# Values of a dilated attention in six chunks of 512 weight columns, queries and keys laid out by head, softmax minimum in one operation

## The chip, the cores and the metric

The kernel runs on one core of a Trainium2 chip. The metric is the device time of one execution in microseconds (us), lower is better. Engines are called as in the profile: PE (TensorE, its weight load apart as PEld), DVE (VectorE), ACT (ScalarE), POOL (GpSimd), SP (SyncE, which issues nearly all transfers).

## The reference, cut to what matters

Four half layers on 256 tokens of width 1024: a mixer of neighbourhood and latent attention, an MLP, a mixer of dilated attention (the odd mixer), an MLP. The change touches the odd mixer alone:

```python
DIL_PAIRS = ((128, 1), (512, 4), (2048, 16)); DIL_HEADS = 16; HEAD_DIM = 64

def dilated_attention(q, k, v):            # b, s, 3 groups, 16 heads, 64
    offsets = [jnp.arange(-(w // 2), w // 2 + 1, d) for (w, d) in DIL_PAIRS]
    ...
        for gi in range(g):
            sc = einsum(q_blk[:, :, gi], k_sel) * scale      # keys at the group's offsets
            sc = jnp.where(valid, sc, NEG_INF)
            m = jnp.max(sc, axis=-1, keepdims=True); e = jnp.exp(sc - m); z = sum(e)
            outs.append(einsum(e / z, v_sel)); lses.append(m + jnp.log(z))
        wgt = softmax(stack(lses), axis=0)
        out = sum(wgt * stack(outs), axis=0)

def odd_mixer(xn, w_in, w_o, cos_f, sin_f):
    hcat = (xn @ w_in).reshape(b, s, DIL_GROUPS, 3, DIL_HEADS, HEAD_DIM)
    q = apply_rope(hcat[:, :, :, 0], cos_f, sin_f)
    k = apply_rope(hcat[:, :, :, 1], cos_f, sin_f)
    v = hcat[:, :, :, 2]
    return dilated_attention(q, k, v) @ w_o
```

The weighting by the groups' sums makes the three groups of a head one softmax over the keys of all three, which is how the kernel computes it.

## The kernel before, in words

All weights come in as float32 and are split on the chip: ACT casts a piece to its high part `whi` (L176), DVE subtracts it for the low part `wlo` (L177). A product is then either three matmuls (`mm3`, L180 to L182, tokens as the stationary side) or, for queries and keys, a pair of one 512-column and one 256-column matmul per 128 input features (`mm2`, L186 and L187). A weight is one transfer on SP's queue into one of 4 buffers `raw`, split in 4 pieces, two weights ahead of its use, into one of 3 split buffers. The list `specs` fixes the order of the weights.

The odd mixer works in 8 units of two heads. A unit has three weights of queries and keys (`w_oqk`: first the queries and keys of group 0, q0, then the queries of groups 1 and 2, q12, then their keys, k12; four steps of 8 matmuls each) and two weights of values (`w_ov`: four steps of 12 matmuls each, 384 columns: two heads in three groups). After each product of queries or keys the halves are joined (ACT copy L193, DVE add L194); after each second one comes the rotation: four transfers `sw<-qk` on SP, multiplications on DVE (L850, L851), and the sum (L853, or L856 for q12 and k12). Values are scaled out of PSUM in L818 (DVE) and L821, L822 (ACT).

The attention of unit u-1 is laid between the steps of unit u by `weave`, which deals a list of side steps evenly between the main steps. Its parts are: `scores` (L201 for group 0, L881 for the small products of groups 1 and 2), inside it the product with the values of unit u-2 (`mix`, L917 and L922), then for each of 2 token tiles and 2 heads a softmax, and four `turn`s (three transposes L902 and a copy `pts`, L904, on DVE or ACT). A softmax is: scaled minimum with the mask on DVE (L889, the minimum is of the negated scores), exponential on ACT (L893), reciprocal on DVE (L894), scaling on ACT (L895). The small products of group g go to the score bank `ss[i, g]`, so a head's scores lie in three places, and its minimum is taken in three operations, each of which begins with the result of the one before:

```python
for n, (o, cs) in enumerate(((ss[i, j][:, 0:T], slice(0, T)), (ss[i, 0][:, at(j)], at(0)), (ss[i, 1][:, at(j)], at(1)))):
    nc.vector.tensor_tensor_reduce(out=sn[:, cs], in0=o, in1=mask[:, i, cs], ...,
                                   scalar=mn[:, n - 1:n] if n else 3e38, accum_out=mn[:, n:n + 1])
```

The attention of unit 7 lies between the steps of the output projection. PSUM is 8 banks, 4 named `w` (scores, transposes) and 4 named `acc` (products of weights, mix). The order of instructions on each engine is not the program's: a scheduler rearranges it by a model of its own.

Of the kernel before, what the change touches and what calls it, by code (L numbers as in the profile page):

```python
# [16 lines left out]
F32 = mybir.dt.float32  # L17
# [22 lines left out]
WPARTS = 4  # L40
NORM_PRIO = 300


@with_exitstack
def trunk(ctx, tc, a, out):
# [739 lines left out]
    def odd(op, xT, s):  # L785
# [8 lines left out]
        def unit_tiles(u):  # L794
            d = {}
            for n, shape, dt in (("q0", [P, 2, 2, T], F32R), ("q12", [P, 2, T], F32), ("k12", [P, 2, T], F32),
                                 ("v0", [P, NT, P], F32), ("v12", [P, 4, P], F32)):
                d[n] = op.tile(shape, dt, tag=n, name=n, bufs=2)
            return d

        def value_steps(d):

            wt, acc = [], {}

            def gemm(i, half):
                if len(wt) <= half:
                    wt.append(weight())
                if half == 0:
                    acc[i] = bank("acc")
                pq = acc[i]  # L810
                wh, wl = wt[half]
                for k in range(4):
                    ws = slice(k * 384, k * 384 + 384)
                    kk = 4 * half + k
                    mm3(pq[:, 0:384], xh[:, kk, tok(i)], xl[:, kk, tok(i)], wh[:, ws], wl[:, ws], kk == 0, kk == KT - 1)
            def out(i):
                pq, ri = acc[i], column(r[0], i)
                nc.vector.tensor_scalar(d["v0"][:, i, :], pq[:, 0:P], ri, None, ALU.mult)  # L818
                for c in range(2):
                    rows = slice(64 * c, 64 * c + 64)  # L820
                    nc.scalar.activation(d["v12"][0:64, 2 * i + c, :], pq[rows, P:2 * P], AF.Copy, scale=ri[rows])  # L821
                    nc.scalar.activation(d["v12"][64:P, 2 * i + c, :], pq[rows, 2 * P:3 * P], AF.Copy, scale=ri[rows])  # L822

            return [lambda i=i, h=h: gemm(i, h) for i in range(NT) for h in range(2)], [lambda i=i: out(i) for i in range(NT)]
# [34 lines left out]

        def all_values(d):  # L860
            g, o = value_steps(d)
            return [g[0], lambda: run_all([g[1], o[0]]), g[2], lambda: run_all([g[3], o[1]])]

        turned = {}

        def attention(u, d, other, pause=2):
# [4 lines left out]
            def scores():  # L871
                ss = {(i, j): bank("w") for i in range(NT) for j in range(2)}
                for i in range(NT):
                    two_heads([ss[i, j][:, 0:T] for j in range(2)], d["q0"], tok(i))
                at = lambda n: slice(T + 64 * n, T + 64 * n + 64)
                for i in range(NT):
                    for j in range(2):
                        for c in range(2):
                            for g in range(2):
                                pb, own = slice(64 * g, 64 * g + 64), slice(i * P + 64 * c, i * P + 64 * c + 64)  # L880
                                nc.tensor.matmul(ss[i, g][64 * c:64 * c + 64, at(j)], d["q12"][pb, j, own], d["k12"][pb, j, own],  # L881
                                                 start=True, stop=True)
                other()
                for i in range(NT):
                    for j in range(2):
                        sn, pp = scratch([384], "sn"), scratch([384], "pp")
                        mn, z, rz = (work.tile([P, n], F32, tag=v, name=v, bufs=4) for v, n in (("dmn", 3), ("dz", 1), ("drz", 1)))
# [20 lines left out]

        def mix(u, d, out_tag):
            pvo = bank(out_tag)  # L910
            for i in range(NT):
                pts = [turned.pop((u, i, j)) for j in range(2)]
                at = i * P
                for kk in range(NT):
                    for j in range(2):
                        cs = slice(64 * j, 64 * j + 64)
                        nc.tensor.matmul(pvo[cs, tok(i)], d["v0"][:, kk, cs], pts[j][:, kk, :], start=kk == 0, stop=False)  # L917
                for c in range(2):
                    qs = slice(64 * c, 64 * c + 64)
                    for j in range(2):  # L920
                        cs = slice(64 * j, 64 * j + 64)
                        nc.tensor.matmul(pvo[cs, at + 64 * c:at + 64 * c + 64], d["v12"][:, 2 * i + c, cs], pts[j][:, 2, qs],  # L922
                                         start=False, stop=c == 1)
            split(*halves(mixed[u // 4][:, u % 4]), pvo[:, 0:T])

        d, nd = unit_tiles(0), unit_tiles(1)
        v0, v_out = value_steps(d)
        run_all(v0)
        r = [rstd(s)]
# [7 lines left out]
        run_all(first[2:])  # L937
        weave(qk_steps(nd) + all_values(nd), attention(0, d, lambda: None, 3), 3)
        for u in range(2, 8):
            pd, d, nd = d, nd, unit_tiles(u)  # L940
            side = attention(u - 1, d, lambda: mix(u - 2, pd, "acc"))

            weave(qk_steps(nd) + all_values(nd), side + [lambda: mix(6, d, "acc")] if u == 7 else side)
        accs, wo = open_accs(), {}
        side = attention(7, nd, lambda: None) + [lambda: mix(7, nd, "w")]
        weave([f for k in range(6) for f in out_steps(accs, mixed, wo, k)], side)
# [54 lines left out]
def _layout(i):  # L1001
# [14 lines left out]
    wo = i["od_w_in"][0].reshape(D, 3, 3, 8, 2, HD)  # L1016
    cols = [(0, 0, 0), (0, 0, 1), (0, 1, 0), (0, 1, 1), (1, 0, 0), (2, 0, 0),
            (1, 0, 1), (2, 0, 1), (1, 1, 0), (2, 1, 0), (1, 1, 1), (2, 1, 1)]
    qk = np.stack([wo[:, g, s, :, j] for g, s, j in cols], 2).reshape(KT, P, 8, 3, 2, P)
    d["w_oqk"] = f(qk.transpose(2, 3, 1, 4, 0, 5).reshape(8, 3, P, WCH))  # L1020
    d["w_ov"] = f(wo[:, :, 2].reshape(2, 4, P, 3, 8, P).transpose(4, 0, 2, 1, 3, 5).reshape(8, 2, P, 4 * 384))
    d["w1"] = f(i["mlp_w1"].reshape(2, KT, P, 16, 256).transpose(0, 3, 2, 1, 4).reshape(2, 16, P, WCH))
# [35 lines left out]
```

## Time and profile before

| what | value |
|---|---|
| median of 3 runs | 744.25 us (744.05 to 745.09) |
| the profiled execution, its own time | 743.78 us |
| its span in the trace | 742.0 us |
| PE busy | 733.4 us (99%) |
| PEld busy | 644.5 us (87%) |
| DVE busy | 551.5 us (74%) |
| ACT busy | 461.7 us (62%) |
| POOL busy | 6.0 us (1%) |
| HBM read | 127.68 MB |

The span is what the trace covers; the execution's own time has 1.78 us more around it. Busy shares are means over all four half layers. The odd mixer lies about between 290 and 575 us of the span.

### The profile page before, as it was taken

The numbers are of one execution on the slowest core, as the hardware profiler recorded it, in microseconds if no ns is written. First come the engines' busy times: TensorE is split into PE (matmuls) and PEld (weight loads), VectorE is DVE, ScalarE is ACT, GpSimd is POOL, SyncE is SP. The second block draws the span as 40 slices with busy tenths as digits, with TensorE's granted clock in tenths as the row PEclk, the third lists the DMA queues.
The fourth block names the chain that finished last, engine by engine and source line by source line (L and its number), as shares of the span: only waits on it lengthen the run. The fifth ranks groups of instructions, "written<-read, shape, count | busy, mean of one in ns | idle before, by whom it ended". The sixth has DMA issues, their size and how long they took to land.

```text
span 742.0 us, 12701 instructions
## 1 busy us (share of the span) xinstructions
PE 733.4 (99%) x4764; PEld 644.5 (87%) x4764; DVE 551.5 (74%) x1248; ACT 461.7 (62%) x1032; POOL 6.0 (1%) x16
## 2 busy tenths in 40 slices
PE   8999999999999999999999999999999999999996
PEld 6998998888888888989899899898998888888885
DVE  6798869666665666998888988888769665665664
ACT  7679867554554546758776766877667544554541
POOL 0100000000000000000000000000000000000000
PEclk9999999999999999999999999999999999999999
DMA  8976334555555554574655555457553546455501
GB/s 296 336 207 220 117 118 164 190 208 182 179 206 185 177 178 150 198 257 150 211 195 185 177 190 189 167 175 240 201 199 126 215 170 208 171 189 190 184 24 57
DMA packets 28108, 136.88 MB, mean 184 GB/s; under 512 B 4496, under 2 KB 7056, under 8 KB 14992
## 3 DMA queue, kind: packets, MB, share of 16 engines
q1 hardware_dynamic: 27760, 135.81, 53.6%
q8 instruction: 37, 0.61, 0.3%
q10 hardware_dynamic: 288, 0.28, 0.1%
q14 instruction: 23, 0.19, 0.1%
HBM read 127.68 MB, written 1.05 MB: 173 GB/s over the span
## 4 chain that ended last, share of the span: by engine, by line
PE 94%; ACT 1%; DMA 1%; issue 1%; DVE 1%; SPq 0%; POOLq 0%; POOL 0%; DVEq 0%
PE w L186 16%; PE acc L180 14%; PE acc L181 14%; PE acc L182 14%; PE acc L186 12%; PE w L187 8%; PE acc L187 6%; PE w L902 1%; PE w L201 1%; PE acc L917 1%; PE w L714 1%; PE w L730 1%; DMA raw<-in_w_v 1%; PE w L881 1%; PE w L180 1%
## 5 line engine op out<-in xcount | busy, mean ns | idle before, releaser
L177 DVE TENSOR_TENSOR wlo<-raw,whi 128x512 fp32r<-128x512 f32 (+3 forms) x488 | 304.0, 663 | 71.5 <-ACT whi L176 70.0
L176 ACT CAST whi<-raw 128x512 fp32r<-128x512 f32 (+3 forms) x488 | 264.3, 601 | 80.3 <-issue 70.1
L186 PE MATMUL w<-xT,whi 128*128 128x512 f32 x512 | 179.4, 394 | 0.0
L186 PE MATMUL acc<-xT,whi 128*128 128x512 f32 x384 | 137.2, 401 | 0.0
L187 PE MATMUL w<-xT,wlo 128*128 128x256 f32 x512 | 132.9, 280 | 0.0
L186 PEld LDWEIGHTS w<-xT,whi 128*128 128x128 f32 x512 | 93.6, 187 | 18.3
L187 PEld LDWEIGHTS w<-xT,wlo 128*128 128x128 f32 x512 | 96.1, 188 | 5.5
L187 PE MATMUL acc<-xT,wlo 128*128 128x256 f32 x384 | 99.7, 280 | 0.0
L180 PE MATMUL acc<-whi,h 128*128 128x512 f32 x250 | 98.4, 393 | 0.0
L181 PE MATMUL acc<-wlo,h 128*128 128x512 f32 x250 | 97.8, 391 | 0.0
L182 PE MATMUL acc<-whi,h 128*128 128x512 f32 x250 | 97.4, 390 | 0.0
L186 PEld LDWEIGHTS acc<-xT,whi 128*128 128x128 f32 x384 | 69.9, 188 | 12.7
L193 ACT COPY up<-w 128x256 f32<-128x256 f32 x64 | 23.8, 372 | 88.5 <-PE w L186 88.5
L187 PEld LDWEIGHTS acc<-xT,wlo 128*128 128x128 f32 x384 | 72.2, 188 | 3.7
L194 DVE TENSOR_TENSOR up<-up,w 128x256 f32<-128x256 f32 x64 | 26.8, 419 | 63.0 <-ACT up L193 62.3
L180 PE MATMUL acc<-whi,xT 128*128 128x384 f32 (+2 forms) x160 | 56.2, 351 | 0.5 <-ACT whi L176 0.5
L181 PE MATMUL acc<-wlo,xT 128*128 128x384 f32 (+2 forms) x160 | 55.7, 348 | 0.5 <-DVE wlo L177 0.3
L182 PEld LDWEIGHTS acc<-whi,h 128*128 128x128 f32 x250 | 47.0, 188 | 10.2
L181 PEld LDWEIGHTS acc<-wlo,h 128*128 128x128 f32 x250 | 47.0, 188 | 9.7
L182 PE MATMUL acc<-whi,xT 128*128 128x384 f32 (+2 forms) x160 | 55.2, 345 | 0.0
L180 PEld LDWEIGHTS acc<-whi,h 128*128 128x128 f32 x250 | 46.9, 188 | 9.1
L181 PEld LDWEIGHTS acc<-wlo,xT 128*128 128x128 f32 x160 | 30.1, 188 | 3.1 <-DVE wlo L177 2.1
(195 smaller groups left out, 1040.9 us busy)
## 6 DMA issues: line engine op xcount, KB each, us to landing
raw<-in_w SPq DMA_DIRECT2D x64, 1024.0 KB, 4.8
raw<-in_w_oqk SPq DMA_DIRECT2D x24, 1024.0 KB, 5.1
raw<-in_w_ov SPq DMA_DIRECT2D x16, 768.0 KB, 4.8
sw<-qk SPq DMA_DIRECT2D x96, 64.0 KB, 3.1
raw<-in_w_qk SPq DMA_DIRECT2D x4, 1024.0 KB, 10.8
raw<-in_w_oe SPq DMA_DIRECT2D x4, 1024.0 KB, 6.6
raw<-in_w_oo SPq DMA_DIRECT2D x4, 1024.0 KB, 5.4
bias<-in_rpb SPq DMA_DIRECT2D x8, 256.0 KB, 5.3
```

The source lines that it names most:

```text
L176: a = nc.scalar.copy(hi, src).ins
L177: return a, (eng or nc.vector).tensor_tensor(lo, src, hi.bitcast(F32), op=ALU.subtract).ins
L180: nc.tensor.matmul(o, sh, mh, start=first, stop=False)
L181: nc.tensor.matmul(o, sh, ml, start=False, stop=False)
L182: nc.tensor.matmul(o, sl, mh, start=False, stop=last)
L186: both = lambda: nc.tensor.matmul(o, sh, m.rearrange("p v n -> p (v n)"), start=first, stop=last)
L187: low = lambda: nc.tensor.matmul(o[:, 0:T], sl, m[:, 0, :], start=False, stop=False)
L193: nc.scalar.copy(dst, o[:, T:2 * T])
L194: nc.vector.tensor_tensor(dst, dst, o[:, 0:T], op=ALU.add)
L201: nc.tensor.matmul(o[j], qk[pb, 0, a, ts], qk[pb, 1, b, :], start=n == 0, stop=n == 2)
L714: nc.tensor.transpose(pt[:, b * P:(b + 1) * P], pp[:, b // 2, (b % 2) * P:(b % 2 + 1) * P], ident)
L730: nc.tensor.matmul(pvo[64 * j:64 * j + 64, o], v[:, kk, h * 64:(h + 1) * 64], pts[:, 2 * j + kk, :], start=kk == 0, stop=kk == NT - 1)
```

## The change

The values' weight is laid out by unit and group in one row of 24 blocks of 128 columns, and cut in 6 chunks of 512 columns (four blocks, so one and a third units each) in place of 8 of 384. `OV_CHUNKS` says which unit's steps hold a chunk: units 3 and 7 hold none. So a chunk makes values of two units, and `unit_values` keeps up to four units' values at a time. The rows of q12 and k12 are laid out with the head as the half of the partitions, where it was the group; with it all scores of a head j lie in one bank `ss[i, j]`, and the minimum is one operation over 384 columns.

```diff
+OV_CHUNKS = ((0,), (1,), (2,), (), (3,), (4,), (5,), ())
...
-        ov = [(a["w_ov"][u, j], 4 * 384) for j in range(2)]
+        ov = [(a["w_ov"][c, j], WCH) for c in OV_CHUNKS[u] for j in range(2)]
         oqk = [(a["w_oqk"][u, j], WCH) for j in range(3)]
         specs.extend(oqk + ov if u else ov + oqk)
...
+        def unit_values(u):
+            if u not in values:
+                values[u] = [op.tile(shape, F32, tag=n, name=n, bufs=4) for n, shape in (("v0", [P, NT, P]), ("v12", [P, 4, P]))]
+            return values[u]
+
+        def value_steps(chunk):
...
                 for k in range(4):
-                    ws = slice(k * 384, k * 384 + 384)
+                    ws = slice(k * 512, k * 512 + 512)
                     kk = 4 * half + k
-                    mm3(pq[:, 0:384], xh[:, kk, tok(i)], xl[:, kk, tok(i)], wh[:, ws], wl[:, ws], kk == 0, kk == KT - 1)
+                    mm3(pq, xh[:, kk, tok(i)], xl[:, kk, tok(i)], wh[:, ws], wl[:, ws], kk == 0, kk == KT - 1)
             def out(i):
                 pq, ri = acc[i], column(r[0], i)
...
+                for n in range(4):
+                    u, g = divmod(4 * chunk + n, 3)
+                    (v0, v12), cs = unit_values(u), slice(n * P, n * P + P)
+                    if g == 0:
+                        nc.vector.tensor_scalar(v0[:, i, :], pq[:, cs], ri, None, ALU.mult)
+                    else:
+                        for c in range(2):
+                            rows = slice(64 * c, 64 * c + 64)
+                            nc.scalar.activation(v12[64 * g - 64:64 * g, 2 * i + c, :], pq[rows, cs], AF.Copy, scale=ri[rows])
...
+        def all_values(u):
+            steps = []
+            for c in OV_CHUNKS[u]:
+                g, o = value_steps(c)
+                steps += [g[0], lambda g=g, o=o: run_all([g[1], o[0]]), g[2], lambda g=g, o=o: run_all([g[3], o[1]])]
+            return steps
...
-                            for g in range(2):
-                                pb, own = slice(64 * g, 64 * g + 64), slice(i * P + 64 * c, i * P + 64 * c + 64)
-                                nc.tensor.matmul(ss[i, g][64 * c:64 * c + 64, at(j)], d["q12"][pb, j, own], d["k12"][pb, j, own],
-                                                 start=True, stop=True)
+                            for j in range(2):
+                                pb, own = slice(64 * j, 64 * j + 64), slice(i * P + 64 * c, i * P + 64 * c + 64)
+                                nc.tensor.matmul(ss[i, j][64 * c:64 * c + 64, T + 64 * g:T + 64 * g + 64], d["q12"][pb, g, own],
+                                                 d["k12"][pb, g, own], start=True, stop=True)
...
-                        for n, (o, cs) in enumerate(((ss[i, j][:, 0:T], slice(0, T)), (ss[i, 0][:, at(j)], at(0)), (ss[i, 1][:, at(j)], at(1)))):
-                            nc.vector.tensor_tensor_reduce(out=sn[:, cs], in0=o, in1=mask[:, i, cs], op0=ALU.add, op1=ALU.min,
-                                                           scale=-(HD ** -0.5), scalar=mn[:, n - 1:n] if n else 3e38,
-                                                           accum_out=mn[:, n:n + 1])
-                        mn = mn[:, 2:3]
+                        nc.vector.tensor_tensor_reduce(out=sn, in0=ss[i, j][:, 0:384], in1=mask[:, i, :], op0=ALU.add, op1=ALU.min,
+                                                       scale=-(HD ** -0.5), scalar=3e38, accum_out=mn)
```

The scheduler answers to the changed code with another order at some places. In the changed file a line of the odd mixer stands some 10 lines lower (L201 is L202, L881 is L894, L902 is L912, L917 and L922 are L927 and L932, L186 and L187 are L187 and L188, L176 and L177 are L177 and L178, L194 is L195, L851 is L862, L856 is L867, L889 is L901, L904 is L914).

The first place is the attention of unit 3 on PE, between the steps of unit 4. Before, after the last k12 product of unit 3 come the four value steps of unit 3 and two steps of unit 4; then:

```order
L187 MATMUL acc<-xT,wlo 128x256
L201 MATMUL w<-q_4228 128x256 x12
L881 MATMUL w<-k_4230,q_4229 64x64 x16
L917 MATMUL acc<-pts,v_3841 64x128 x4
L922 MATMUL acc<-pts,v_3842 64x64 x4
L917 MATMUL acc<-pts,v_3841 64x128 x4
L922 MATMUL acc<-pts,v_3842 64x64 x4
L186 MATMUL acc<-xT,whi 128x512
```

The group 0 scores, the small products and the mix of unit 2 stand in a row, and the first transposes come 32 matmuls later. In the changed kernel unit 3 has no value steps, and only one step (8 matmuls) lies between its last k12 product and this:

```order
L188 MATMUL acc<-xT,wlo 128x256
L202 MATMUL w<-q_4224 128x256 x12
L927 MATMUL acc<-pts,v_3795 64x128 x4
L932 MATMUL acc<-pts,v_3796 64x64 x4
L927 MATMUL acc<-pts,v_3795 64x128 x4
L932 MATMUL acc<-pts,v_3796 64x64 x4
L187 MATMUL acc<-xT,whi 128x512
...
L894 MATMUL w<-k_4226,q_4225 64x64 x16
```

The small products (L894), which need k12, have been put off by 32 matmuls of unit 4. Then 17 more matmuls of queries and keys follow, and the transposes stand so:

```order
L187 MATMUL acc<-xT,whi 128x512
L912 MATMUL w<-ident,pp 128x128 x3
L188 MATMUL acc<-xT,wlo 128x256
L187 MATMUL acc<-xT,whi 128x512
L188 MATMUL acc<-xT,wlo 128x256
L187 MATMUL acc<-xT,whi 128x512
L188 MATMUL acc<-xT,wlo 128x256 x2
L187 MATMUL acc<-xT,whi 128x512
L912 MATMUL w<-ident,pp 128x128 x9
L187 MATMUL acc<-xT,whi 128x512
```

The second, third and fourth turn stand in a row, 7 matmuls after the first; before, 24 matmuls lay between two turns. The last row begins a product in a new bank `acc`. On DVE the end of the same softmax, with the copies of the turns and the joining of products, stands so in the changed kernel:

```order
L904 RECIPROCAL drz<-dz 128x1
L901 ISA sn,dmn<-w,mask 128x384
L901 ISA dmn 128x1
L914 COPY pts<-w 128x384
L904 RECIPROCAL drz<-dz 128x1 x2
L914 COPY pts<-w 128x384 x2
L195 TENSOR_TENSOR qk<-qk,acc 128x256 x2
```

Two joining additions (L195), which free banks `acc`, stand behind the last reciprocals and three copies of turned probabilities. The third place is DVE ahead of L894: from the joining of unit 3's last k12 product (first row) to its k12 (last row):

```order
L195 TENSOR_TENSOR qk<-qk,acc 128x256
L862 TENSOR_TENSOR sw<-sw,sinT 128x512
L178 TENSOR_TENSOR wlo<-raw,whi 128x512
L867 TENSOR_TENSOR q_4225<-r_4440,sw 128x512
L178 TENSOR_TENSOR wlo<-raw,whi 128x512 x2
L861 TENSOR_TENSOR r_4512<-qk,cosT 128x512
L178 TENSOR_TENSOR wlo<-raw,whi 128x512
L178 TENSOR_TENSOR oa<-acc,oa 128x256
L862 TENSOR_TENSOR sw<-sw,sinT 128x512
L867 TENSOR_TENSOR k_4226<-r_4512,sw 128x512
```

Nine operations of 512 columns and one of 256 stand between the joining and the end of k12. The attention of unit 7, in the output projection, has the same form: L894 stands 58 projection matmuls of 256 columns, the mix of unit 6 and L202 behind unit 7's last k12 product; then 25 matmuls, turn, 7, turn, 6, turn, 24, turn.

## Rows read from the trace of the kernel before

**Rows 1.** The page's chain that ended last, shares by engine.

```profile
PE 94%; ACT 1%; DMA 1%; issue 1%; DVE 1%; SPq 0%; POOLq 0%; POOL 0%; DVEq 0%
```

**Rows 2.** Waits of PE, 290 to 575 us: total us, times, longest us.

```profile
PE w L881 <- DVE k L856: 0.2, 1, 0.2
```

**Rows 3.** Stretches: us; PE, PEld, DVE, ACT, POOL busy (count); granted clock; DMA share; GB/s.

```profile
407.20:437.00 29.80, 29.80 (x234) 27.09 (x233) 25.15 (x70) 21.29 (x51) 0.00 (x0) 1.00 0.57 186
...
398.56:402.62 4.06, 4.06 (x24) 4.06 (x23) 3.36 (x6) 2.45 (x5) 0.00 (x0) 1.00 0.75 237
403.31:407.12 3.81, 3.81 (x24) 3.81 (x23) 1.61 (x5) 3.26 (x8) 0.00 (x0) 1.00 0.56 184
726.79:730.87 4.08, 4.08 (x19) 3.38 (x18) 2.43 (x5) 1.40 (x4) 0.54 (x1) 1.00 0.00 0
20.53:23.81 3.28, 3.28 (x15) 2.64 (x14) 2.38 (x7) 2.97 (x8) 0.71 (x1) 1.00 1.08 355
357.84:358.52 0.68, 0.68 (x7) 0.64 (x5) 0.45 (x1) 0.68 (x2) 0.00 (x0) 1.00 0.03 12
```

**Rows 4.** Groups by form, PE, 290 to 575 us: busy us, mean ns, idle before.

```profile
L180 PE MATMUL acc<-whi,xT 128*128 128x384 f32 x128 | 44.0, 343 | 0.0
```

**Rows 5.** Timeline of PE, an attention: start us, us, instruction.

```profile
379.00 0.98 PE L201 MATMUL w<-q 64*128 64x256 f32 x12
379.91 0.69 PE L881 MATMUL w<-k,q 64*64 64x64 f32 x32
380.53 0.66 PE L917 MATMUL acc<-pts,v 128*64 128x128 f32 x8
...
382.02 0.50 PE L186 MATMUL acc<-xT,whi 128*128 128x512 f32 x1
382.36 0.28 PE L187 MATMUL acc<-xT,wlo 128*128 128x256 f32 x1
382.48 0.39 PE L186 MATMUL acc<-xT,whi 128*128 128x512 f32 x1
382.71 0.28 PE L187 MATMUL acc<-xT,wlo 128*128 128x256 f32 x1
```

**Rows 6.** Timeline in unit 1, small products and first minimum; waits in brackets.

```profile
327.38 0.69 PE L881 MATMUL w<-k,q 64*64 64x64 f32 x32 [0.20 <-DVE k L856]
...
328.31 0.41 DVE L889 CUSTOM_DVE_ANT_0 sn<-w,mask 128x256 f32<-128x256 f32 x1
```

**Rows 7.** Timeline of DVE, the same attention as Rows 5.

```profile
379.32 2.48 DVE L177 TENSOR_TENSOR wlo<-raw,whi 128x512 fp32r<-128x512 f32 x4
...
383.69 0.41 DVE L889 CUSTOM_DVE_ANT_0 sn<-w,mask 128x256 f32<-128x256 f32 x1
384.03 0.08 DVE L889 DVE_READ_ACCUMULATOR2_ANT dmn<- 128x1 f32 x1
...
389.05 0.54 DVE L904 COPY pts<-w 128x384 f32<-128x384 f32 x1
389.51 0.74 DVE L194 TENSOR_TENSOR qk<-qk,acc 128x256 f32<-128x256 f32 x2
```

**Rows 8.** Timeline of ACT, the same softmax.

```profile
383.80 0.62 ACT L893 ACTIVATE pp<-sn,dmn 128x384 f32<-128x384 f32 x1 [1.29 <-DVE dmn L889]
...
384.74 0.62 ACT L895 ACTIVATE pp<-pp,drz 128x384 f32<-128x384 f32 x1 [0.23 <-DVE drz L894]
385.26 0.61 ACT L893 ACTIVATE pp<-sn,dmn 128x384 f32<-128x384 f32 x1
...
389.36 0.62 ACT L895 ACTIVATE pp<-pp,drz 128x384 f32<-128x384 f32 x1
```

**Rows 9.** First value product behind the last k12 product, its k12; transfers: KB, us.

```profile
368.77 0.34 PE L180 MATMUL acc<-whi,xT 128*128 128x384 f32 x1
...
378.73 0.68 DVE L856 TENSOR_TENSOR k<-r,sw 128x512 f32<-128x512 f32 x1
...
sw<-qk SPq DMA_DIRECT2D x96, 64.0 KB, 3.1
```

More of the change, by code (lines that the diff above doesn't have):

```diff
@@ L795, in unit_tiles @@
             d = {}
-            for n, shape, dt in (("q0", [P, 2, 2, T], F32R), ("q12", [P, 2, T], F32), ("k12", [P, 2, T], F32),
-                                 ("v0", [P, NT, P], F32), ("v12", [P, 4, P], F32)):
+            for n, shape, dt in (("q0", [P, 2, 2, T], F32R), ("q12", [P, 2, T], F32), ("k12", [P, 2, T], F32)):
                 d[n] = op.tile(shape, dt, tag=n, name=n, bufs=2)
             return d
-        def value_steps(d):
+        values = {}
+        def unit_values(u):
[3 more added lines that the diff above has]
+        def value_steps(chunk):
             wt, acc = [], {}
@@ L874, in scores @@
                     two_heads([ss[i, j][:, 0:T] for j in range(2)], d["q0"], tok(i))
[L875 removed]
                 for i in range(NT):
[L877 removed]
+                    for g in range(2):
                         for c in range(2):
[L879 to L882 removed]
+                            for j in range(2):
+                                pb, own = slice(64 * j, 64 * j + 64), slice(i * P + 64 * c, i * P + 64 * c + 64)
+                                nc.tensor.matmul(ss[i, j][64 * c:64 * c + 64, T + 64 * g:T + 64 * g + 64], d["q12"][pb, g, own],
+                                                 d["k12"][pb, g, own], start=True, stop=True)
                 other()
@@ L907, in attention, with mix @@
             return [scores] + [wait] * pause + [f for i in range(NT) for j in range(2) for f in (lambda i=i, j=j: turn(i, j), wait)]
-        def mix(u, d, out_tag):
-            pvo = bank(out_tag)
+        def mix(u, out_tag):
+            pvo, (v0, v12) = bank(out_tag), values.pop(u)
             for i in range(NT):
@@ L916, in mix @@
                         cs = slice(64 * j, 64 * j + 64)
-                        nc.tensor.matmul(pvo[cs, tok(i)], d["v0"][:, kk, cs], pts[j][:, kk, :], start=kk == 0, stop=False)
+                        nc.tensor.matmul(pvo[cs, tok(i)], v0[:, kk, cs], pts[j][:, kk, :], start=kk == 0, stop=False)
                 for c in range(2):
@@ L921, in mix @@
                         cs = slice(64 * j, 64 * j + 64)
-                        nc.tensor.matmul(pvo[cs, at + 64 * c:at + 64 * c + 64], d["v12"][:, 2 * i + c, cs], pts[j][:, 2, qs],
+                        nc.tensor.matmul(pvo[cs, at + 64 * c:at + 64 * c + 64], v12[:, 2 * i + c, cs], pts[j][:, 2, qs],
                                          start=False, stop=c == 1)
@@ L926, in odd @@
         d, nd = unit_tiles(0), unit_tiles(1)
-        v0, v_out = value_steps(d)
-        run_all(v0)
+        products, v_out = value_steps(0)
+        run_all(products)
         r = [rstd(s)]
@@ L937, in odd @@
         run_all(first[2:])
-        weave(qk_steps(nd) + all_values(nd), attention(0, d, lambda: None, 3), 3)
+        weave(qk_steps(nd) + all_values(1), attention(0, d, lambda: None, 3), 3)
         for u in range(2, 8):
-            pd, d, nd = d, nd, unit_tiles(u)
-            side = attention(u - 1, d, lambda: mix(u - 2, pd, "acc"))
-            weave(qk_steps(nd) + all_values(nd), side + [lambda: mix(6, d, "acc")] if u == 7 else side)
+            d, nd = nd, unit_tiles(u)
+            side = attention(u - 1, d, lambda: mix(u - 2, "acc"))
+            weave(qk_steps(nd) + all_values(u), side + [lambda: mix(6, "acc")] if u == 7 else side)
         accs, wo = open_accs(), {}
-        side = attention(7, nd, lambda: None) + [lambda: mix(7, nd, "w")]
+        side = attention(7, nd, lambda: None) + [lambda: mix(7, "w")]
         weave([f for k in range(6) for f in out_steps(accs, mixed, wo, k)], side)
```

17 lines of the change are left out of this document (5 added, 12 removed).

## The prediction

> **What bounds the kernel now.** I read the chain that ended last first: 94% of it is PE [rows 1]. Then the odd mixer alone, since the change lies there. [...] The waits of PE between 290 and 575 us come to a single one of 0.2 us [rows 2]. So in this stage time is PE's list of instructions, and nothing else is waited for. What the change saves elsewhere counts only if PE later waits there; what it saves in PE's list counts in full; and any new wait of PE counts in full as well.
>
> **The values.** A unit has 48 matmuls of 384 columns. The form's group shows 128 of them for L180 [rows 4]; with L181 and L182, which stand in the same loop, 384 in all, 8 units of 48. From the start of the first to the start of the 24th of one run lie 4.06 us, so 176.6 ns from one to the next; in the second run, from its second matmul to its last, 3.81 us for 22 steps, 173.2 ns (the counts also take in the tails of those before; second and third of [rows 3]). Half of each: 24 x 0.1766 + 24 x 0.1732 = 8.40 us per unit, 67.2 us in 8 units.
>
> The change makes of them 6 x 48 = 288 matmuls of 512 columns: the same columns, 96 matmuls fewer. No row has this very product. Two have near ones: in the MLP, 18 steps in 4.08 us, 226.7 ns; in the even mixer, with the same tokens on the stationary side, 14 steps in 3.28 us, 234.3 ns (fourth and fifth of [rows 3]). From 173.2 at 384 columns to 226.7 at 512 is 0.417 ns per column, so some 160 of the 173.2 ns go with the columns, and 13 ns with the matmul. In the two busier runs this part is larger, 16.6 ns (384 columns) and 20.9 ns (512), with the DMA share at 0.75 and 1.08 where it was 0.56 and 0.00 in the tighter ones. I take 229 ns, the columns' 213.4 and a little over the mean of the two 384-column runs' rest (15): 288 x 0.229 = 66.0 us, so **-1.2 us**. The bounds: 288 x 0.2267 = 65.3 (-1.9 us) and 288 x 0.2343 = 67.5 (+0.3 us).
>
> That a matmul costs some 13 ns beside its columns is this trace's number. [...]
>
> **The softmax minimum.** Three operations and three reads of the result become one of each, 32 times. One of 256 columns takes 0.34 us to the next start (383.69 to 384.03 in [rows 7]), a 384-column copy 0.46 (389.05 to 389.51 there), which I take for the new one. The two small ones are shorter than the 256-column one, so a softmax saves less than 2 x 0.34 + 0.34 - 0.46 = 0.56 us of DVE, a unit less than 2.2. On PE's path this is worth nothing: no turn waits now [rows 2]. Its cover is the 4.65 us per unit in which DVE is idle (the first of [rows 3]). The other layout of q12 and k12 gives the same 16 small products in the same number, and the scaling out of PSUM has as many operations as before. The values' weight has the same bytes in 12 transfers for 16, and where a unit spent 24 x 0.175 = 4.2 us on a weight of values it now spends 24 x 0.229 = 5.5 for one that is a third larger: the same rate. All these at nothing, hidden by PE.
>
> **The units without values.** They move the load: unit 3 and unit 7 have only their 12 query and key steps. What was hidden behind value steps is not any more, in two places: the attention of unit 3 (inside unit 4) and that of unit 7 (inside the output projection).
>
> First, k12. Before, its rotation could use the whole value part: the value products began at 368.77, and k12 was done at 378.73 + 0.68 = 379.41, 10.6 us later [rows 9]; PE took it at 379.91 [rows 5]. Now, in unit 4: 8 matmuls at a mean of 0.175 us (a pair takes 382.71 - 382.36 = 0.35 [rows 5]) 1.40; L202 0.91 and the mix 1.49 (379.00 to 379.91 and 380.53 to 382.02 in [rows 5]); 32 matmuls 5.6: L894 comes 9.4 us after the last k12 product. In DVE's list nine operations of 512 columns at 0.62 (four take 2.48 [rows 7]) and one of 256, 0.34, lie between the joining and k12: 5.9 us, and about 0.9 for the joining itself (two additions take 0.74 [rows 7]; ACT's copy is taken as long as one). 6.8 us, 2.6 before PE asks for it. By the transfers: 0.9, 3.1 to landing [rows 9] and two operations 1.2 make 5.2, so the four issues may spread over 4.2 us. I cost it at **0**. If it takes the 10.6 us of before, PE waits 1.2. In the output projection, 12 matmuls of 256 columns at 0.12 (382.36 to 382.48 in [rows 5]), mix, L202 and 46 more give 1.4 + 1.5 + 0.9 + 5.5 = 9.3 behind the last product: the same answer.
>
> Second, the turns of unit 4. I walk from the end of L894 (0). First minimum 0.31 later, as 328.31 stands to the 328.00 at which PE went on in unit 1 (327.38 and 0.62, the pitch of rows 5) [rows 5, 6]; first exponential at about 0.87. From an exponential to its scaling 0.94, one ACT operation per 0.52 (383.80 to 384.74 to 385.26 in [rows 8]). DVE splits a weight piece (0.62) ahead of the second and the third minimum, which delays the next exponentials, and ACT takes two exponentials before the first scaling; the four scalings end at 3.1, 4.3, 5.4 and 5.9. PE comes to the first turn after 17 matmuls, 3.0: it goes on at 3.2. A turn costs PE 0.68 - 0.35 = 0.33 (the last of [rows 3], and [rows 5]); 7 matmuls 1.2; so the second turn starts at 4.8, the third must wait until 5.4, the fourth until 6.0, done at 6.2. Behind it a product begins in a fresh bank `acc`, which is freed by the joining of an earlier one; ACT has that copy behind its last scaling, DVE the addition behind three copies of turns (0.46 each): 6.9. With no wait PE would be there at 3.0 + 0.3 + 1.2 + 0.8 = 5.3. **+1.5 us**. Behind it waits PE's whole list. Lower bound, if the bank is free in time: 6.2 - 5.3, +0.8 or a little more. Upper bound: in the trace the scalings end 389.36 + 0.62 - 383.80 = 6.2 us after the first exponential [rows 8], with other work between, 1.2 later than in my walk: +2.7.
>
> In the output projection the first turn comes after 25 matmuls, 3.0, where the scaling ends at 3.1; the second at 4.4, the third at 5.4, just as they are done; the fourth 2.9 later. **+0.2 us**, between 0 and 0.8. In the other units nothing of this changes: turns lie 16 to 24 matmuls apart, 2.8 to 4.2 us, against an ACT step of 0.52.
>
> **The sum.** -1.2 + 1.5 + 0.2 = +0.5 us. The profiled execution took 743.78 us, a span of 742.0 and 1.78 around it; so 744.3. The runs' median, 744.25, is 0.47 above it: **744.7 us**. A measurement of this kernel can tell about 0.2% (1.5 us) from no change, so this is "no change".
>
> **The rivals.**
> *Slower, the burst in unit 4.* The shortened cover doesn't hold: either ACT's chain is as long as now (6.2 us) with the turns in a row behind it, 2.7 + 0.8 - 1.2 = +2.3, 746.5 us; or k12 needs its 10.6 us at both places, 1.5 + 0.2 + 2.4 - 1.2 = +2.9, 747.1. For it: the trace has such lengths. Against: they were long because nobody waited; DVE's list ahead of k12 and of the minima is now shorter. It decides from 2.7 us of waits on: 2.7 - 1.2 = 1.5, 0.2%.
> *The matmuls give nothing back.* The rest beside the columns grows with the width, as the 234.3 ns of the even mixer say: +0.3 + 1.7 = +2.0, 746.2. For it: same tokens stationary, same operand types. Against: there the transfers were at a share of 1.08, in the odd mixer at 0.57.
> *Faster, no wait.* The softmax of unit 4 is in time (DVE is free of 8 small operations, and the pieces between may be split earlier), and the pitch is the MLP's 226.7: -1.9, 742.4 us. For it: the clean pitch; PE has waited for nothing here so far. Against: 17 matmuls between scores and first turn where there were 32, and three turns in a row. It needs waits under 0.4 us in all to be told from no change.
>
> **How the numbers follow.** Forecast (waits of 0.5 to 2.7 us, a pitch of 0.226 to 0.231) 0.54; burst 0.16; no gain from the matmuls 0.10; faster 0.20. The range goes from the faster case, 742.3, to the late k12, 747.2; what is left out are waits beyond both bounds. Faster by over 0.2%: 0.20; slower by over 0.2%: 0.16 + 0.10 = 0.26; within: 0.54.
>
> **What would show it.** In the profile after: value matmuls of 512 columns at 0.227 to 0.231 us from start to start; waits of PE for ACT's `pp` in the turns (L912) of unit 4, and one for DVE (`qk`) at the product behind them, together 0.8 to 2.7 us; none, or little, at L894; unit 3 and unit 7 about 8.4 us shorter than 29.8, the others 11.0 - 8.4 = 2.6 longer, unit 4 more; DVE about 2 us less busy per unit, with PE's share unchanged. Wrong would make me: a turn that waits in each unit, a wait for weights at the first chunk behind an empty unit, or a pitch outside 0.226 to 0.235.

## The result and the profile after

The changed kernel takes 747.18 us (median of 7 runs, 746.15 to 747.43), the kernel before in the same session 744.69 us (7 runs, 744.05 to 745.09): a ratio of 1.0032, 95% interval 1.0022 to 1.0041, so 1.6 to 3.1 us slower. 744.7 was forecast. A few executions took far longer than all others of the same kernel (up to 1459 us) and are left out of the medians and ratios.

The page of the changed kernel, busy times and the chain that ended last:

```profile
PE 735.4 (99%) x4668; PEld 633.0 (85%) x4668; DVE 541.8 (73%) x1104; ACT 458.4 (61%) x1016; POOL 5.7 (1%) x16
...
PE 90%; ACT 3%; DVE 2%; DMA 2%; issue 1%; SPq 1%; POOLq 0%; POOL 0%; DVEq 0%; ACTq 0%
```

PE has 96 instructions fewer and is busy 2 us longer, and its share of the chain has gone from 94% [rows 1] to 90%. What PE waits for in the odd mixer (us in total, times, longest), where [rows 2] had one line:

```profile
PE acc L187 <- DVE qk L195: 0.5, 1, 0.5
PE w L894 <- DVE k L867: 0.3, 1, 0.3
PE w L912 <- ACT pp L905: 0.2, 1, 0.2
```

Stretches of the changed kernel, columns as in [rows 3]: from one attention's scores to the next for unit 3 (no values), unit 4 and unit 5, and below them 47 steps of value products of 512 columns:

```profile
389.10:410.49 21.39, 21.39 (x186) 18.61 (x185) 16.67 (x39) 16.48 (x40) 0.00 (x0) 1.00 0.52 173
410.49:444.74 34.25, 33.58 (x235) 27.70 (x234) 28.27 (x60) 20.15 (x47) 0.00 (x0) 1.00 0.57 185
444.74:477.35 32.61, 32.61 (x234) 27.69 (x233) 25.28 (x53) 22.94 (x55) 0.00 (x0) 1.00 0.54 186
...
432.00:443.00 11.00, 11.00 (x48) 8.85 (x47) 8.25 (x15) 6.62 (x14) 0.00 (x0) 1.00 0.65 223
```

Two things are to be seen. The pitch of the value products (the time from one start to the next) is 11.00 / 47 = 234.0 ns, at the upper bound of the prediction, not the 229 taken. And unit 4 is 34.25 - 32.61 = 1.64 us longer than a regular unit with a chunk; PE is idle for 34.25 - 33.58 = 0.67 us of it.

The whole odd mixer, cut at the starts of the scores of each attention (L201 or L202 in PE's timeline, from the last up-product of the first MLP to the first of the second; the first row holds the first MLP's last down products, 17.9 us), in us:

| stretch | before | after | values_only | lead_unit4 | xt_high |
|---|---|---|---|---|---|
| to scores 0 | 50.57 | 53.31 | 53.33 | 53.31 | 52.96 |
| scores 0 to 1 | 24.49 | 27.48 | 28.06 | 27.49 | 27.19 |
| scores 1 to 2 | 29.79 | 32.61 | 32.61 | 32.61 | 32.35 |
| scores 2 to 3 (unit 3) | 29.79 | 21.39 | 21.39 | 25.60 | 21.42 |
| scores 3 to 4 (unit 4) | 29.79 | 34.25 | 40.35 | 28.84 | 33.65 |
| scores 4 to 5, and 5 to 6, each | 29.79 | 32.61 | 32.61 | 32.61 | 32.35 |
| scores 6 to 7 (unit 7) | 31.44 | 23.10 | 23.10 | 23.10 | 23.12 |
| from scores 7 | 26.33 | 26.45 | 27.21 | 26.45 | 26.45 |
| odd mixer | 281.80 | 283.81 | 291.26 | 282.62 | 281.84 |

(The last three columns are experiments, below.) The odd mixer is 2.0 us longer. The rest of the difference of the two profiled executions lies ahead of it: until the first scores of the even mixer the kernel before took 40.54 us and the changed one 42.11. This start is the same code; over thirteen profiles of this study it took 40.54 to 42.30 us, in no order that goes with a change, while from there to the first down product of the MLP all took 89.4 to 89.6 us, and the MLPs repeat within 0.3 us. So small effects below are read from the odd mixer's length, and the run times tell them less sharply.

### The profile page after: what moved, and what is told of

It reads as the page before. It is cut to its first block, busy times and chain, and to the rows that moved or that the text cites. A ratio compares the mean times of both kernels' runs of the same rounds, so it can differ in the third digit from the quotient of the medians.

```text
span 745.7 us, 12284 instructions
## 1 busy us (share of the span) xinstructions
PE 735.4 (99%) x4668; PEld 633.0 (85%) x4668; DVE 541.8 (73%) x1104; ACT 458.4 (61%) x1016; POOL 5.7 (1%) x16
## 4 chain that ended last, share of the span: by engine, by line
PE 90%; ACT 3%; DVE 2%; DMA 2%; issue 1%; SPq 1%; POOLq 0%; POOL 0%; DVEq 0%; ACTq 0%
PE w L187 16%; PE acc L181 15%; PE acc L182 14%; PE acc L183 14%; PE acc L187 9%; PE w L188 8%; PE acc L188 5%; PE w L912 1%; DMA sw<-qk 1%; PE w L202 1%; PE w L715 1%; DVE wlo L178 1%; PE w L731 1%; DMA raw<-in_w_c 1%; PE acc L927 1%
## 5 line engine op out<-in xcount | busy, mean ns | idle before, releaser
L178 DVE TENSOR_TENSOR wlo<-raw,whi 128x512 fp32r<-128x512 f32 (+2 forms) x472 | 302.5, 682 | 68.4 <-ACT whi L177 67.1
L177 ACT CAST whi<-raw 128x512 fp32r<-128x512 f32 (+2 forms) x472 | 262.4, 616 | 94.5 <-issue 77.3
L187 PE MATMUL w<-xT,whi 128*128 128x512 f32 x512 | 179.4, 394 | 0.0
L187 PE MATMUL acc<-xT,whi 128*128 128x512 f32 x384 | 138.2, 401 | 0.5 <-DVE qk L195 0.5
L188 PE MATMUL w<-xT,wlo 128*128 128x256 f32 x512 | 132.8, 280 | 0.0
L187 PEld LDWEIGHTS w<-xT,whi 128*128 128x128 f32 x512 | 93.5, 187 | 18.3
L188 PEld LDWEIGHTS w<-xT,wlo 128*128 128x128 f32 x512 | 96.1, 188 | 5.5
L188 PE MATMUL acc<-xT,wlo 128*128 128x256 f32 x384 | 99.8, 280 | 0.0
L187 PEld LDWEIGHTS acc<-xT,whi 128*128 128x128 f32 x384 | 70.3, 188 | 13.9 <-DVE qk L195 0.7
L194 ACT COPY up<-w 128x256 f32<-128x256 f32 x64 | 23.9, 373 | 88.4 <-PE w L187 88.4
L188 PEld LDWEIGHTS acc<-xT,wlo 128*128 128x128 f32 x384 | 72.2, 188 | 3.6
L195 DVE TENSOR_TENSOR up<-up,w 128x256 f32<-128x256 f32 x64 | 26.8, 419 | 62.9 <-ACT up L194 62.3
L181 PE MATMUL acc<-whi,xT 128*128 128x512 f32 (+1 forms) x128 | 51.3, 401 | 1.7 <-ACT whi L177 1.7
L182 PE MATMUL acc<-wlo,xT 128*128 128x512 f32 (+1 forms) x128 | 50.8, 397 | 0.2 <-DVE wlo L178 0.2
L183 PE MATMUL acc<-whi,xT 128*128 128x512 f32 (+1 forms) x128 | 50.4, 394 | 0.0
L833 ACT ACTIVATE v<-acc,rstd 64x128 f32<-64x128 f32 x64 | 23.2, 363 | 21.0 <-PE acc L183 15.0
```

The costliest lines, as they stand in the source:

```text
L177: a = nc.scalar.copy(hi, src).ins
L178: return a, (eng or nc.vector).tensor_tensor(lo, src, hi.bitcast(F32), op=ALU.subtract).ins
L181: nc.tensor.matmul(o, sh, mh, start=first, stop=False)
L182: nc.tensor.matmul(o, sh, ml, start=False, stop=False)
L183: nc.tensor.matmul(o, sl, mh, start=False, stop=last)
L187: both = lambda: nc.tensor.matmul(o, sh, m.rearrange("p v n -> p (v n)"), start=first, stop=last)
```

## The experiments

**The softmax edit alone** (kernel before, with q12 and k12 by head and the one-operation minimum):

```diff
-                    for j in range(2):
+                    for g in range(2):
                         for c in range(2):
-                            for g in range(2):
+                            for j in range(2):
...
-                        for n, (o, cs) in enumerate(((ss[i, j][:, 0:T], slice(0, T)), (ss[i, 0][:, at(j)], at(0)), (ss[i, 1][:, at(j)], at(1)))):
...
+                        nc.vector.tensor_tensor_reduce(out=sn, in0=ss[i, j][:, 0:384], in1=mask[:, i, :], op0=ALU.add, op1=ALU.min,
+                                                       scale=-(HD ** -0.5), scalar=3e38, accum_out=mn)
```

> The kernel before with the layout of q12 and k12 by head and the one-operation minimum; values as before (eight times 384 columns). Theory (PE's list alone sets the time of this stage): PE's list is the same to the instruction, so within 0.3 us of the kernel before, although DVE is busy about 2 us less per unit; PE waits at most once more for 0.2 us. Rival (the layout or the minimum costs or gains on PE's path, by the other alternation of row halves in the small products or by earlier turns): 0.5 us or more to either side.

744.71 us against 744.61, ratio 1.0000 (0.9991 to 1.0009); the odd mixer takes 282.05 us, 0.25 more than before. One unit of it:

```profile
380.36:410.15 29.79, 29.79 (x234) 27.07 (x233) 23.02 (x52) 21.66 (x52) 0.00 (x0) 1.00 0.55 186
```

DVE is busy 23.02 us where it was 25.15 [rows 3], with 52 instructions for 70, and the unit is as long as before. The edit saves 2.1 us of DVE per unit, and none of it reaches the time, as the theory said.

**The chunks alone** (the changed kernel with the old layout and the three minima, so the difference above taken back):

> The changed kernel with the old layout and the three-operation minimum: only the six chunks of 512 columns and the two units without values. Theory (the values carry all of the difference): 2.0 to 3.0 us above the kernel before, as much as the changed kernel or a little more, since a longer softmax makes the row of turns in unit 4 wait longer. Rival (part of the loss comes from the softmax edit): at most 1.2 us above the kernel before.

754.09 us, ratio 1.0128 (1.0112 to 1.0143): 9.5 us slower, more than any theory had. The table above puts 6.1 of the 7.45 us beyond the changed kernel's odd mixer into unit 4. Its waits of PE in the odd mixer:

```profile
PE w L916 <- ACT pp L909: 1.7, 2, 1.1
PE acc L187 <- DVE qk L195: 1.6, 1, 1.6
PE w L895 <- DVE k L867: 1.1, 2, 0.8
```

Three stretches inside its unit 4, columns as above:

```profile
425.00:430.00 5.00, 1.74 (x8) 1.17 (x9) 4.21 (x15) 5.00 (x13) 0.00 (x0) 0.76 0.21 87
430.00:435.00 5.00, 5.00 (x19) 4.34 (x18) 2.69 (x6) 1.11 (x4) 0.00 (x0) 0.56 0.37 92
435.00:440.00 5.00, 5.00 (x27) 4.18 (x26) 3.32 (x6) 2.57 (x7) 0.00 (x0) 1.00 0.73 236
```

And two neighbouring 512-column matmuls of query and key pairs on PE's timeline, in the second of these stretches (start, us):

```profile
430.16 0.63 PE L187 MATMUL acc<-xT,whi 128*128 128x512 f32 x1
...
430.80 0.63 PE L187 MATMUL acc<-xT,whi 128*128 128x512 f32 x1
```

From 425 to 430 us PE is busy for 1.74 of 5 us: it stands at a turn, then at another, then at a product whose bank the joining has not freed. Over this stretch the granted clock is 0.76 and over the next 0.56, though PE is busy without a gap from 429.35 on; over the third, to 440 us, it is 1.00. In the second stretch a pair of matmuls takes 0.64 us where it takes 0.35 at 1.00 [rows 5]. So this burst, some 4 us of waits, costs some 2.4 more in slow matmuls (nine pairs, from 429.35 to 434.89 us, take 5.54 us for 9 x 0.35 = 3.15). In the changed kernel PE is idle for 0.67 us at the same place, and the clock stays at 1.00. The one-operation minimum, worth nothing by itself, is worth 7 us next to the chunks.

**Banks in turn** (the changed kernel with the tokens' two tiles inside the loop over input features):

```diff
-                for k in range(4):
+                for k in (2 * part, 2 * part + 1):
                     ...
+                    for i in range(NT):
+                        mm3(acc[i], xh[:, kk, tok(i)], xl[:, kk, tok(i)], wh[:, ws], wl[:, ws], kk == 0, kk == KT - 1)
```

> The changed kernel, its value products in another order: for each 128 input features first the three matmuls of token tile 0, then those of tile 1, so that every third matmul changes its PSUM bank, where 24 in a row go to one bank now. All else on PE stands in the same order. Theory (the 234 ns of the value products come from 24 matmuls of a whole bank's 512 columns in a row into one bank; in the MLP every third changes bank and the pitch is 228): pitch 227 to 229 ns, 288 x 6 ns = 1.7 us less than the changed kernel. Rival (the 234 ns belong to these operands, tokens of xT as the stationary side, or to the chip's load in this stage): pitch stays at 233 to 235 ns, the time within 0.3 us of the changed kernel.

```profile
431.41:442.41 11.00, 11.00 (x48) 8.85 (x47) 9.93 (x17) 5.16 (x10) 0.00 (x0) 1.00 0.71 238
```

746.94 us, ratio 1.0033 (1.0020 to 1.0045), and 234.0 ns as before: the theory of the one bank falls.

**A later attention in unit 4** (three main steps ahead of it):

```diff
-            weave(qk_steps(nd) + all_values(u), side + [...] if u == 7 else side)
+            weave(qk_steps(nd) + all_values(u), side + [...] if u == 7 else side, 0 if OV_CHUNKS[u - 1] else 3)
```

> The changed kernel, but in the unit behind a unit without values the attention's steps begin three main steps later: on PE the scores of unit 3 stand 24 matmuls later, its turns 19, 8 and 24 matmuls apart, none in a row. Theory (the row of turns in unit 4 waits 1.2 us for the softmax and the joining, and costs 0.3 us more by standing in a row): 1.2 to 1.5 us less than the changed kernel, no wait of PE for ACT's probabilities or DVE's joining in unit 4. Rival (the waits move to the new places of the small products or of the turns): within 0.4 us of the changed kernel.

745.66 us, ratio 1.0013 (1.0004 to 1.0022), 1.5 us under the changed kernel; the odd mixer is 1.2 us shorter. Units 3 and 4 take 25.60 + 28.84 = 54.44 us, where they took 55.64. Of PE's waits in the odd mixer one is left:

```profile
PE w L894 <- DVE k L867: 0.3, 1, 0.3
```

(it is that of unit 1, as in [rows 6]). So the row of turns cost 1.2 us. A unit without and one with a chunk would take 21.39 + 32.61 = 54.00, so 0.44 stays.

**The chunks alone, with the later attention:**

> The chunks of values with the old layout and the three-operation minimum, and in unit 4 the lead of three main steps. Theory (the 9.5 us of the chunks with the old minimum were one chain in unit 4: PE waits about 5 us for k12, probabilities and joinings, and the granted clock falls for about 5 us after it; the one-operation minimum is worth that much there and nothing elsewhere): with the lead the clock stays full in unit 4, and the time is within 1.5 us of the changed kernel with the same lead, 745.7 to 747.2. Rival (the longer softmax costs in all units or in the output projection with the chunks): 749 or more.

747.96 us, ratio 1.0047 (1.0033 to 1.0061), between the two. Two stretches of unit 4, at the same times as above:

```profile
425.00:430.00 5.00, 5.00 (x33) 4.33 (x32) 4.48 (x20) 5.00 (x13) 0.00 (x0) 1.00 0.37 154
430.00:435.00 5.00, 4.90 (x25) 3.90 (x24) 3.86 (x11) 4.62 (x12) 0.00 (x0) 1.00 0.78 249
```

PE's waits in the odd mixer (a smaller one, on weights, left out):

```profile
PE w L895 <- DVE k L867: 1.5, 3, 0.7
```

The clock stays at 1.00, and the time falls by 6.1 us, from 754.09 to 747.96. But it is 2.3 us above the changed kernel with the same lead, not within 1.5. The odd mixers differ by 3.1 us (285.75 and 282.62): 0.6 from scores 0 to 1, 0.9 in unit 4 and 1.6 from scores 7 on. k12 is late at these three attentions, 1.5 us in all where it was 0.3; that the three minima keep DVE busy longer is the likely reason and was not traced, and 1.9 of the 3.1 us are not explained. "Worth nothing elsewhere" was wrong: the smaller softmax is also worth something at each attention with a short cover.

**A still later attention, in the output projection too** (five steps in unit 4, three there):

```diff
-            weave(qk_steps(nd) + all_values(u), side + [...] if u == 7 else side)
+            weave(qk_steps(nd) + all_values(u), side + [...] if u == 7 else side, 0 if OV_CHUNKS[u - 1] else 5)
...
-        weave([f for k in range(6) for f in out_steps(accs, mixed, wo, k)], side)
+        weave([f for k in range(6) for f in out_steps(accs, mixed, wo, k)], side, 3)
```

> The changed kernel; the attention's steps begin five main steps later in unit 4 and three later in the output projection. On PE the scores and the small products of unit 3 stand in a row again but for half of the mix, 24 and 16 matmuls between its turns; in the output projection the small products still stand apart, turns 26, 1, 19 and 12 matmuls apart. Theory (what is left of the loss with the shorter lead, 0.8 us in the odd mixer, is the price of attentions broken in two pieces, about 0.3 us each, at unit 4 and the output projection): 0.2 to 0.5 us less than with the shorter lead, 745.2 to 745.5. Rival (two turns one matmul apart in the output projection wait for ACT): 0.5 us or more above the shorter lead.

746.84 us, ratio 1.0029 (1.0019 to 1.0039): 1.2 us above the shorter lead, so the rival, or another. The same kernel once more, for its profile:

> The kernel with the lead of five steps in unit 4 and three in the output projection once more, for a profile at the full clock. Theory (its 747.0 us, 1.4 above the shorter lead, come from the output projection, where the second turn stands one matmul behind the first, ahead of its softmax): waits of 1.0 to 1.6 us of PE for ACT's probabilities there, unit 4 without a wait. Rival (unit 4's turns, now 24, 16 and 20 matmuls apart with the mix cut in two, wait): more than 0.5 us of waits in unit 4.

```profile
PE w L894 <- DVE k L867: 1.0, 3, 0.4
```

Neither. The turns hardly wait (0.24 us at one). PE waits for k12 three times, in units 1 and 4 and in the output projection, since the scheduler now lets the small products follow the scores sooner. The odd mixer takes 283.81 us, 1.2 more than with the shorter lead, of which these waits explain 0.7 (0.3 stood there before); the rest was not traced. Units 3 and 4 take 0.3 us more than with the shorter lead, unit 7 and the output projection 0.9.

**xT in another place of SBUF** (the build gives the bytes per partition: xT at 25920, the split weights from 120288 on; the kernel here has xT behind the weights, at 153056, and these from 103904 on; the scratch tiles, `work`, and the buffers `raw`, which lie between, move down by 16384 bytes as well):

```diff
+    xp = ctx.enter_context(tc.tile_pool(name="xp", bufs=1))
     ps = ctx.enter_context(tc.tile_pool(name="ps", bufs=4, space=PSUM))
-        return pair_tile(act, KT, "xT", 1, "xpair")
+        return pair_tile(xp, KT, "xT", 1, "xpair")
```

> The changed kernel with the tile xT (the stationary side of the value products) in another place of SBUF: behind the split weights (from 153056 bytes per partition) where it was ahead of them (25920), in the even and the odd mixer; the order on PE is the same to the instruction. Theory (the 234 ns come from where the stationary and the moving operand lie to each other; the run with alternating banks left it at 233.8 to 234.3 ns): the pitch of the 512-column value products moves by 3 ns or more, towards the 227 ns of the MLP at best, the time by 0.9 to 2.0 us with it. Rival (the place has no part in it): 233 to 235 ns, the time within 0.4 us of the changed kernel.

```profile
430.49:441.17 10.68, 10.68 (x49) 8.82 (x47) 8.13 (x15) 6.61 (x14) 0.00 (x0) 1.00 0.69 229
```

744.81 us, ratio 1.0006 (0.9996 to 1.0015). The pitch is 10.68 / 47 = 227.2 ns. The odd mixer loses 1.97 us, the two MLPs 0.3 together. The order of instructions is the same to the last, so it is the place of something in SBUF. Two more places of xT:

> The changed kernel with xT moved by 16384 bytes per partition, to 42304, still far ahead of the split weights, which stay where they were (120288 on). Theory (it is the region, near to the weights or behind them, that counts): pitch of the value products stays at 233 to 235 ns. Rival (any other place than the first does): 227 to 229 ns.

> The changed kernel with xT directly ahead of the split weights, at 103904, the weights where they were (120288 on). Theory (the place of xT counts, not that of the weights, which moved as well where xT was put behind them): 227 to 229 ns. Rival (the move of the weights by 16384 bytes did it): 233 to 235 ns.

The same 47 steps, first with xT at 42304, then with xT at 103904, directly ahead of the weights; in both the weights lie where the changed kernel has them:

```profile
431.07:442.07 11.00, 11.00 (x48) 8.85 (x47) 8.25 (x15) 6.62 (x14) 0.00 (x0) 1.00 0.63 221
```

```profile
429.71:440.37 10.66, 10.66 (x49) 8.82 (x47) 8.13 (x15) 6.62 (x14) 0.00 (x0) 1.00 0.69 226
```

At 42304 it is 234.0 ns, at 103904 226.8 (single runs, 746.50 and 744.20 us). So not every move of xT does it, and it isn't that of the weights: with the stationary side at 26 or 42 KB and the moving side at 120 KB and above, the product of 512 columns has some 7 ns more than with both above 100 KB.

That it is the place of xT alone is not shown. With xT at 103904 `work` and `raw` lie 16384 bytes lower, as with xT at 153056; with xT at 42304 they lie where they lay. A stretch of the first MLP shows that a product can gain without any move of its own operands: 23 steps of the down products, whose operands (`h` and the weights) keep their places in all three kernels, and in which PE does not read xT. First the changed kernel, then xT at 42304, then xT at 103904:

```profile
142.74:147.99 5.25, 5.25 (x25) 4.32 (x23) 4.12 (x7) 2.97 (x6) 0.00 (x0) 1.00 0.35 147
...
142.03:147.28 5.25, 5.25 (x25) 4.32 (x23) 4.12 (x7) 2.98 (x6) 0.00 (x0) 1.00 0.37 154
...
141.83:147.05 5.22, 5.22 (x24) 4.32 (x23) 4.12 (x7) 2.98 (x6) 0.00 (x0) 1.00 0.35 149
```

The pitch is 228.3, 228.3 and 227.0 ns, and all 12 such stretches of this MLP repeat it within 0.4 ns. No run moves `work` and `raw` without xT.

**The kernel before with xT behind the weights, and the best of the changed one:**

> The kernel before with xT behind the split weights in SBUF and nothing else. Theory (the place acts on any product with xT as the stationary side, the 384-column ones less, since half of their runs stand at 173 ns already): the 384-column runs at 176.6 ns go to 173 to 174, the MLP's 228.3 to 227.0, in all 1.0 to 1.8 us below the kernel before, so that the wider products are worth at most 0.5 us once the place is right. Rival (only products of a whole bank's 512 columns are slowed by the place): 384-column pitch unchanged, at most 0.9 us below the kernel before.

> The changed kernel with both: xT behind the split weights in SBUF, and the lead of three steps in unit 4. Theory (the two losses, 1.9 to 2.2 us of pitch and MLP with the place, 1.2 to 1.4 us of unit 4's turns, are independent): 743.4 to 743.8, about 1 us below the kernel before. Rival (they overlap): 744.3 or more.

The first 384-column run of a unit of the kernel before with xT moved:

```profile
399.48:403.50 4.02, 4.02 (x25) 4.02 (x23) 3.32 (x6) 2.45 (x5) 0.00 (x0) 1.00 0.74 241
```

4.02 / 23 = 174.7 ns for 176.6, and a unit of 29.71 us for 29.79: narrow products gain 2 ns in half of their runs, not 3, so the theory is right in kind and half in size. The kernel takes 743.45 us against 744.60, ratio 0.9980 (0.9971 to 0.9990). The changed kernel with xT moved and the lead takes 744.01, ratio 0.9993 (0.9984 to 1.0002), above the 743.4 to 743.8 expected: the two gains in the odd mixer, 1.97 and 1.19 us, come to 2.6 together. Without their starts the two profiles say it the other way by 0.4 us (odd mixer 281.37 and 281.19, the MLPs 0.2), so which is the faster stays open; the kernel before with xT moved is the one that beats both kernels of this case by its runs.

## Why the prediction was right or wrong

**The values: wrong, by its pitch.** 229 ns were taken, between 226.7 (MLP) and 234.3 (even mixer). It is 234.0. By units: a unit of before less one without values is 29.79 - 21.39 = 8.40 us, as forecast; one with a chunk less one without is 32.61 - 21.39 = 11.22. Six times 11.22 is 67.3, eight times 8.40 is 67.2: the forecast gain of 1.2 us is none. (The 67.2 is itself some 0.2 us high: a run of 384 columns at 176.6 ns stands only in units 2 to 6, and in the other three both runs are at 173 to 174, so 67.0.) The step that failed is the choice in the middle: "a little over the mean of the two 384-column runs' rest". The row of the even mixer had the same operands as the new product, in kind and in place, and should have been taken; it was read as a matter of transfers (a DMA share of 1.08). That row moves with the places too. Here are 34 steps of it, first with xT at 42304, then at 103904:

```profile
20.39:28.36 7.97, 7.97 (x36) 6.41 (x35) 6.08 (x15) 6.06 (x13) 1.26 (x2) 1.00 0.81 313
...
20.49:28.23 7.74, 7.74 (x35) 6.38 (x34) 5.85 (x14) 6.11 (x13) 1.26 (x2) 1.00 0.84 327
```

That is 234.4 and 227.6 ns at nearly the same DMA share. So the runs show places in SBUF instead: with xT near the weights, and `work` and `raw` moved with it, the products of the odd mixer stand at 227 ns, and six chunks take 6 x (32.35 - 21.42) = 65.6 us. That is 1.6 us less than the 67.2 of before, but there the narrow products take less too, 8 x (29.71 - 21.42) = 66.3: by the lengths of the units the width is worth 0.7 us in that place and nothing in the other. (By the pitches of single stretches, 174.7 and 173.5 against 227.2 ns, it would be 1.4 us there; which is nearer was not settled.)

**The turns of unit 4: right.** +1.5 us were forecast, 1.64 measured, of which the later attention gives 1.2 back. PE's own idle time shows 0.67 of it; its weight load waits 1.5 us for ACT and for the joining, and in a regular unit for neither:

```profile
PEld w L912 <- ACT pp L905: 0.8, 3, 0.4
PEld acc L187 <- DVE qk L195: 0.7, 1, 0.7
```

PE's timeline of the changed kernel there (start, us; waits in brackets):

```profile
410.49 0.98 PE L202 MATMUL w<-q 64*128 64x256 f32 x12
...
418.71 0.69 PE L894 MATMUL w<-k,q 64*64 64x64 f32 x32
...
422.51 0.55 PE L912 MATMUL w<-ident,pp 128*128 128x128 f32 x3
...
424.07 0.49 PE L912 MATMUL w<-ident,pp 128*128 128x128 f32 x3
...
424.76 1.05 PE L912 MATMUL w<-ident,pp 128*128 128x128 f32 x6 [0.20 <-ACT pp L905]
426.28 0.50 PE L187 MATMUL acc<-xT,whi 128*128 128x512 f32 x1 [0.47 <-DVE qk L195]
```

And DVE and ACT beside it:

```profile
419.57 0.55 DVE L901 CUSTOM_DVE_ANT_0 sn<-w,mask 128x384 f32<-128x384 f32 x1
...
425.81 0.74 DVE L195 TENSOR_TENSOR qk<-qk,acc 128x256 f32<-128x256 f32 x2
```

```profile
420.16 0.62 ACT L903 ACTIVATE pp<-sn,dmn 128x384 f32<-128x384 f32 x1 [0.52 <-DVE dmn L901]
...
424.10 1.11 ACT L905 ACTIVATE pp<-pp,drz 128x384 f32<-128x384 f32 x2
```

The walk counted from the end of L894, 418.71 + 0.62 = 419.33. First exponential 0.83 later (0.87 said), first turn 3.18 (3.2), second 4.74 (4.8), last scaling done at 425.21, so 5.88 (5.9), the product behind the turns 6.95 (6.9), which waits for the additions that start at 425.81. Each step holds to 0.1 us, worked out from durations before the change and the order after it.

**k12: right in unit 4** (PE did not wait there, its weight load 0.3 us; L894 came 418.71 - 410.49 = 8.2 us behind L202's start, and 1.4 more behind the last product), and the 0.3 us at L894 is that of unit 1. But the stretch from scores 0 to 1 grew by 2.99 us, 0.17 more than the other units with a chunk (2.82). 0.1 of it is k12, for which PE waits 0.3 us where it waited 0.2: there too the scheduler moved the small products, which the prediction didn't look at. The other 0.07 is that both runs of 384 columns stood at 173 to 174 ns there before.

**The output projection:** +0.2 forecast, +0.12 measured, no wait of PE.

**The softmax minimum at nothing: right**, 0.0 in the runs by itself. That it was the cover of the burst in unit 4 was not seen: the prediction priced it by the kernel before, where nothing waits for a softmax, and not by the changed one.

**The sum.** Values 0.0 (forecast -1.2), unit 4 +1.6 (+1.5), unit 1 +0.2 (0), output projection +0.1 (+0.2): +1.9 of the 2.0 us by which the odd mixer grew. It is the rival "the matmuls give nothing back", given 0.10, with the forecast's own waits; its price of +2.0 was right. 747.18 lies just inside the range, whose upper end is 747.2, and that is luck: the end was worked out from a k12 late in two places, which did not happen. The start of the profiled execution was long as well, 1.6 us longer than in the profile before; for the other runs that was not traced.

## What to carry to other kernels

Where two rows bound an unknown price, take the row with the same operands in the same places, and not the mean: here that row was 5 ns per matmul worse and exactly right. When an edit takes work out from between two dependent steps (here two units without values), walk the chain that lost its cover step by step with rows of before and the order of after; such a walk can hold to a tenth of a microsecond. An edit that is worth nothing where nobody waits can be worth microseconds next to one that makes somebody wait, so edits that come together are priced together.

## What the runs showed of the hardware that was not expected

- The place of tiles in SBUF changed the pitch of matmuls: 512 columns of float32 at 234.0 ns with xT, the stationary side, at 25920 or 42304 bytes per partition and the moving weights at 120288 and above, 226.8 to 227.2 ns with xT at 103904 or 153056. 384 columns went from 176.6 to 174.7 ns in the first run of a unit and stayed at 173 to 174 in the second. `work` and `raw` moved with it in the two faster places, and the MLP's down products, none of whose operands moved, went from 228.3 to 227.0 ns. What makes it was not found; with the PSUM bank changed every third matmul the pitch stayed at 234.0 ns.
- With the chunks alone the granted clock was 0.76 over the 5 us of unit 4 in which PE was busy for 1.74 us, 0.56 over the next 5 us, in which it was busy throughout, and 1.00 over the 5 us after those. In the changed kernel, with 0.67 us idle in unit 4, it was 1.00 over the whole unit.
- The start of the program, up to the first scores, took 40.5 to 42.3 us in thirteen profiles of code that is the same there but for the place of xT: a spread nearly as large as the whole effect of this change (1.8 and 2.0 us).
